# Splitting weights a chunk ahead and turning modulation rows a call later in a convolution and pooling mixer

## The chip, the cores and the metric

One core of a Trainium2 chip runs the kernel in one launch. The metric is device time in microseconds (us); a smaller one is better. Engines are named as in the profile: PE (TensorE, matmuls), PEld (its weight loads), DVE (VectorE), ACT (ScalarE), POOL (GpSimd), SP (SyncE, which here issues the loads).

## The reference

Two layers of a trunk work on 768 tokens (512 latent and 256 context) of width 1024. Layer 0's mixer is a pooling branch beside a convolution branch, layer 1's an mLSTM beside grouped-query attention, and each is followed by an expert retrieval (PEER). What matters here:

```python
z = h @ w_in                                  # mixer of layer 0: 12 chunks of 128 columns
ya = multiscale_pool(z[..., :D_POOL])         # chunks 0 to 3
a, gt = jnp.split(z[..., D_POOL:], 2, -1)     # chunks 4 to 7 and 8 to 11
u = a * jax.nn.sigmoid(gt)
y = depthwise_conv(u, conv_w)                 # 31 taps along the tokens, per column
out = concat([ya, silu(layer_norm(y))], -1) @ w_out
```

Every sub-layer has a modulation (shift, scale and gate), a linear map of the conditioning vector: for each layer 12 pieces of 512 outputs, each `silu(c) @ mod_w` plus a bias. The layer input h of a mixer is `x * (1 + scale) + shift`.

## The kernel before, in words

Matrices in float32 are split into a high and a low part (`split`: ScalarE casts the high part, L295; VectorE subtracts for the low one, L296), and a product is three matmuls: high by low, high by high, low by high.

**First mixer** (`mixer0`, L425). `zchunk(m)` loads one 128-column weight chunk of 512 KB (`load_chunk`, L311; SP), splits it into `c_hi` and `c_lo`, and runs its 48 matmuls (`mm_chunk`), 24 of 512 and 24 of 256 tokens, into the PSUM tile `zps`. A loop over g = 0 to 3 (L514) runs a value chunk (pa) and a gate chunk (pg), the sigmoid `sg` on ScalarE (L520) and their product `upad` on VectorE (L522, L523). Then the taps of that g start as a generator (`taps`, L466). For g = 1 and 2 a tap is one VectorE operation (L472); for g = 0 it is a scaled copy `ctap` on ScalarE (L476) and an add on GpSimd (L477). The fourth g's taps run on PE later (`taps_pe`, L480, matmuls with scaled identity matrices `cdh` and `cdl`). A second loop (L532) runs the four pool chunks z, copied by ScalarE into `g_acc` and `g_h`; `pooled` (L550) and `taps_pe` follow. `advance(6)` (L499) is called once per chunk, and lets each running tap generator issue up to 4 (g = 0) or 6 (g = 1, 2) taps.

**Modulation** (`mod_piece`, L180). A piece is a load of 2 MB (`modw`), 32 matmuls of two rows by 128 columns (the profile counts each as two records) into `modp`, four ScalarE copies into `mrow` (L195), a PE transpose of `mrow` into `modt` (L71), and a VectorE add of the bias into `modT` (L199), for scales also L201. `modp` and `modt` share two PSUM buffers. The first four pieces come before the first mixer, two more after each g, one after each z chunk: 16 of the 24. Weights for these are held in a ring of three `modw` buffers.

**Second mixer** (`mixer1`, L1108). The last eight pieces are placed by `mod()` (L1308) between the groups of the projection (`tps`, weights `t_hi`, `t_lo`) and the four query chunks (`qps`). Their weights come in quarters of 512 KB through `g_acc` and `g_h`. Queries are normed on DVE, POOL and ACT (`rny`, `qdup`) and transposed on PE (`qaps`).

**Order.** A scheduler places each engine's instructions within the bounds of the program; PSUM buffers, tile rings and the calls of `issue_after` set which of them can move. Each engine then runs its own list in order.

Of the kernel before, what the change touches and what calls it, by code (L numbers as in the profile page):

```python
# [9 lines left out]
F32 = mybir.dt.float32  # L10
# [5 lines left out]
OP = mybir.AluOpType  # L16
AX = mybir.AxisListType

P = 128
D = 1024  # L20
KB = D // P
NLAT, NCTX = 4, 2
NTOK = (NLAT + NCTX) * P
# [30 lines left out]
        "eq": (1.2, 0, 0), "tree": (.8, 0, 0), "gates": (1.0, 0, .6), "none": (0, 0, 0)}  # L54
NEG = -3.0e38
CONV_W = 31
ROPE_F = 16


# [15 lines left out]
def kernel(tc, a, out):  # L75
    nc = tc.nc
    V, S, G, PE, SP = nc.vector, nc.scalar, nc.gpsimd, Tracked(nc.tensor), nc.sync
# [19 lines left out]
    def kt(shape, name, dt=F32):  # L97
        return kp.tile(shape, dt, name=name)


    small = kt([P, a["smalls"].shape[1]], "small")
# [11 lines left out]
    cT, mod_bT = part(KB, 2), part(2, 48)  # L113
    pool_ls, conv_w = part(4), part(4, CONV_W)
    conv_b, conv_g, conv_lb = part(4), part(4), part(4)
    ln_gT, ln_bT = part(3, KB), part(3, KB)

    iota, row = kt([P, P], "iota"), kt([P, 1], "row")
    G.iota(iota, pattern=[[1, P]], base=0, channel_multiplier=0, allow_small_or_imprecise_dtypes=True)
    G.iota(row, pattern=[[1, 1]], base=0, channel_multiplier=1, allow_small_or_imprecise_dtypes=True)  # L120
    ident = kt([P, P], "ident")
# [46 lines left out]
    anchor, loaded, copied = [None], [None], [None]  # L168


    scT = kt([P, KB, 2], "scT")
    S.activation(scT, cT, AF.Silu)
    modT = [kt([P, 48, 2], f"modT{l}") for l in range(2)]
    mrow = [kt([P, P], f"mrow{i}") for i in range(2)]
    mcount = [0]
    for r in mrow:
        G.memset(r, 0.0)

    def mod_piece(l, j, w, pp, tag="small", bufs=2, after=None, queue=SP):

        nb = KB // len(w)
        ps = pp.tile([P, P], F32, name="modp", tag=tag, bufs=bufs)
        for k in range(KB):
            if k % nb == 0:
                with tc.issue_after(after.ins) if after is not None else nullcontext():
                    queue.dma_start(w[k // nb], a["mod_w"][l, j, :, k:k + nb])
            for g in range(4):
                PE.matmul(ps[32 * g:32 * g + 2], scT[:, k, :], w[k // nb][:, k % nb, g * P:(g + 1) * P],
                          start=k == 0, stop=k == KB - 1, tile_position=(0, 32 * g))
        mcount[0] += 1  # L190
        row = mrow[mcount[0] % 2]
        pt = pp.tile([P, P], F32, name="modt", tag=tag, bufs=bufs)
        for g in range(4):
            r = slice(32 * g, 32 * g + 2)
            S.copy(row[r], ps[r])  # L195
        PE.transpose(pt, row, ident)
        pt = pt.rearrange("p (g r) -> p g r", r=32)[:, :, :2]
        dst = modT[l][:, 4 * j:4 * j + 4, :]
        V.tensor_tensor(dst, pt, mod_bT[:, l, 4 * j:4 * j + 4].unsqueeze(2).to_broadcast([P, 4, 2]), op=OP.add)  # L199
        if j // 2 in (1, 4):  # L200
            V.tensor_scalar_add(dst, dst, 1.0)  # L201

    def gate_rows(dst, l, blk, s, wp, pp, tag="small", bufs=2):
        for h in range(2):
# [96 lines left out]
    def mm_chunk(ps, wh, wl, hh, hl, n):  # L301

        for k in range(KB):
            for w, h, first, last in ((wh, hh, k == 0, False), (wh, hl, False, False), (wl, hh, False, k == KB - 1)):
                for o, ln in spans(n):
                    PE.matmul(ps[:, o:o + ln], w[:, k], h[:, k, o:o + ln], start=first, stop=last)
# [5 lines left out]
    def load_chunk(src, wp, bufs=2, tag="c", rbufs=3, parts=()):  # L312
        raw = wp.tile([P, KB, P], F32, name="c_raw", tag=tag + "_raw", bufs=rbufs)
        loaded[0] = SP.dma_start(raw, src)
        wh, wl = parts.pop() if parts else chunk_parts(wp, bufs, tag)
        anchor[0] = split(wh, wl, raw)
        return wh, wl
# [109 lines left out]
    def mixer0(gt):  # L427
        with ExitStack() as es:
# [4 lines left out]
            ppS = pool(e3, "m0psS", 1, PSUM)  # L433
            ppB = pool(e3, "m0psB", 1, PSUM)
            e4 = ExitStack()
            wp = pool(e4, "m0w")
            ea = ExitStack()
            mw = pool(ea, "m0mod", side="right")
            cacc = xp.tile([P, 4, 783], F32, name="cacc")
            hh = wp.tile([P, KB, NTOK], F32R, name="h1h")  # L440
            hl = wp.tile([P, KB, NTOK], F32R, name="h1l")
            segs = ((0, 0, 512), (527, 512, 256))

            def mods(*js):
                for j in js:
                    mod_piece(*divmod(j, 12), [mw.tile([P, KB, 512], F32, name="modw", bufs=3)], ppS, after=loaded[0])

            mods(0, 2, 1, 3)
            for k in range(KB):
                xt = wp.tile([P, NTOK], F32, name="xt", bufs=4)  # L450
                SP.dma_start(xt, a["xT"][:, k])
# [5 lines left out]
            def big():  # L457
                return ppB.tile([P, NTOK], F32, name="zps", tag="big", bufs=3)

            def zchunk(m):  # L460
                wh, wl = load_chunk(a["ab_w_in"][m], wp, 2, "c", 2)
                ps = big()
                mm_chunk(ps, wh, wl, hh, hl, NTOK)
                return ps

            def taps(g, up):  # L466

                V.tensor_scalar(cacc[:, g], up[:, 0:783], conv_w[:, g, 0:1], conv_b[:, g:g + 1],
                                op0=OP.mult, op1=OP.add)
                for k in range(1, CONV_W):  # L470
                    if g in (1, 2):
                        V.scalar_tensor_tensor(cacc[:, g], up[:, k:k + 783], conv_w[:, g, k:k + 1], cacc[:, g],  # L472
                                               op0=OP.mult, op1=OP.add)
                    else:
                        ct = cp.tile([P, 783], F32, name="ctap", bufs=2)
                        S.activation(ct, up[:, k:k + 783], AF.Copy, scale=conv_w[:, g, k:k + 1])  # L476
                        G.tensor_tensor(cacc[:, g], cacc[:, g], ct, op=OP.add)  # L477
                    yield

            def taps_pe(g, uh, ul):  # L480

                ps = big()
                for k in range(CONV_W):
                    w = conv_w[:, g, k:k + 1]
# [12 lines left out]
            running = []  # L497
# [14 lines left out]
                for o in (0, 520, 784):  # L512
                    G.memset(zp[:, o:o + 8], 0.0)
            for g in range(4):  # L514
                pa = zchunk(4 + g)
                advance(6)
                pg = zchunk(8 + g)
                advance(6)
                sg = wp.tile([P, NTOK], F32, name="sg")
                S.activation(sg, pg, AF.Sigmoid)  # L520
                up = ups[g]
                V.tensor_tensor(up[:, 15:527], pa[:, :512], sg[:, :512], op=OP.mult)  # L522
                V.tensor_tensor(up[:, 542:798], pa[:, 512:], sg[:, 512:], op=OP.mult)  # L523
                if g < 3:
                    running.append((taps(g, up), (4, 6, 6)[g]))
                else:
                    uh = cp.tile([P, 813], F32R, name="uph", bufs=1)
                    ul = cp.tile([P, 813], F32R, name="upl", bufs=1)
                    split(uh, ul, up)
                    us.append((g, uh, ul))  # L530
                mods(2 * g + 4, 2 * g + 5)
            for g in range(4):  # L532
                ps = zchunk(g)
                zp = gs[g]
                S.copy(zp[:, 8:520], ps[:, :512])
                S.copy(zp[:, 528:784], ps[:, 512:])
                advance(6)
                mods(12 + g)
            e4.close()
            ea.close()  # L540
            op = Operand(NTOK, "opa", NL)
            e5 = ExitStack()
            wp = pool(e5, "m0p")
# [45 lines left out]
            wp = pool(e5, "m0n")  # L589
# [28 lines left out]
            wp = pool(es, "po")  # L618
            pp = pool(es, "po_ps", 1, PSUM)
# [489 lines left out]
    def mixer1(op, pre, wp, ready, gt):  # L1109
        order = ((4, 5, 0, 1, 2, 3), (5, 4, 3, 2, 1, 0))  # L1110
        with ExitStack() as es:
# [23 lines left out]
            with ExitStack() as e2:  # L1135
                pr = pool(e2, "m1p")
                pp = pool(e2, "m1_ps", 1, PSUM)
# [165 lines left out]
                        else:  # L1303
                            hold(prep_q(t, c0 // DH, ps[:, :n]))

                mods = iter([(1, j) for j in range(4, 12)])

                def mod():  # L1308
                    ws = [gt[x][:, 0].rearrange("p (k n) -> p k n", n=512) for x in ("acc", "h")] * 2
                    mod_piece(*next(mods), ws, pp, "sm", 3)  # L1310

                group("gkv", 0, *CD_FIRST[0], ready[0], (0, 4, 1, 5, 2, 3))
                if MO == 0:
                    seen_groups.add("k")
                group("qa", 0, *CD_FIRST[1], ready[1])
                seen_groups.add("k")
                mod()
                mod()
                group("qa", 256, 1792, 256)
                mod()  # L1320
                group("k", 0, 0, 256)
                mod()
                group("k", 256, 256, 256)
                mod()
                for m in range(H4):
                    wh, wl = load_chunk(a["cd_w_q"][m], wp, 2, "t", 2)
                    ps = pp.tile([P, NL], F32, name="qps", tag="tps", bufs=5)
                    mm_chunk(ps, wh, wl, op.hi, op.lo, NL)
                    S.copy(qT[:, m], ps)
                    if m % 2:  # L1330
                        mod()
                for q_ in later + gates:
                    for _ in q_:
                        pass
                later.clear()
                group("v", 0, 512, 256)
                mod()
                group("v", 256, 768, 256)
                group("o", 0, 1024, 256)
                group("o", 256, 1280, 256)  # L1340
# [3 lines left out]
            op = Operand(NL, "opc", len(DENSE[1]) * P)  # L1344
            with ExitStack() as e2:
                wp = pool(em, "m1b")
                wa = pool(e2, "m1t", side="right")
                SM = [wp.tile([P, NLAT, 2, 2, P], F32, name=f"sm{d}") for d in range(2)]
                pp = pool(e2, "m1b_ps", 1, PSUM)
# [266 lines left out]
    with ExitStack() as es:  # L1616
        gt = gather_state(0, es)
        op = mixer0(gt)
        nxt = peer(op, 0, gt, x_d[1])
    with ExitStack() as es:  # L1620
        gt = gather_state(1, es)
        op = mixer1(*nxt, gt)
# [75 lines left out]
```

## Time and profile before

| | us |
|---|---|
| median of three runs | 3821.45 (3821.12 to 3821.5) |
| the profiled execution's own time | 3821.29 |
| its span in the profile | 3819.5 |
| first mixer, second chunk's end to the start of the PE taps | 147.2 (53.0 to 200.2) |
| second mixer, the projections | 165.4 (2118.5 to 2283.9) |
| PE busy, share of the span | 96% |
| mean granted clock of PE, of full speed | 0.983 |

A time in a timeline counts from the start of the span. Busy time is work of an engine; an engine that runs its list in order waits where the next instruction's input or buffer is not there. In square brackets stands the idle time ahead of an instruction and what ended it. The two expert retrievals take most of the span and are not touched.

### The profile page before, as it was taken

What the parts mean: (1) busy time and instruction counts of PE and PEld (TensorE: products, weight loads), DVE (VectorE), ACT (ScalarE), POOL (GpSimd) and SP (SyncE); (2) the same over time, 40 slices, a digit from 0 to 9 for tenths busy, and PEclk for the clock granted to TensorE, in tenths of its full rate; (3) what the DMA queues carried; (4) which work ended last, traced back from release to release, by engine and by line L of the source; (5) the groups of instructions that cost most, each with busy time, mean ns of one, the idle gap of its engine ahead of it and who ended that gap; (6) DMA issues with size and microseconds to landing.
All of it is one profiled execution on the core that took longest, in us unless ns stands there. A gap on an engine that the chain in (4) does not pass through costs nothing. (4 is left out here: it accounts for less than half of the span.)

```text
span 3819.5 us, 57323 instructions
## 1 busy us (share of the span) xinstructions
PE 3653.0 (96%) x20375; PEld 3165.7 (83%) x20375; DVE 3101.9 (81%) x6574; ACT 1838.8 (48%) x3234; POOL 1715.0 (45%) x1213
## 2 busy tenths in 40 slices
PE   7789999999999999999998999899999999999998
PEld 5668788788888778888887889789999999888776
DVE  4977899999999778889886517588988887688778
ACT  4342322388888733323224434433358998333332
POOL 3300155444454467888860203103422223687773
PEclk9899999999999999999999999899999999999999
DMA  8323499899999989999983430157978889899885
GB/s 318 137 86 123 163 324 329 303 333 360 378 347 356 371 321 346 358 376 362 356 330 129 136 111 1 67 205 270 313 263 320 311 298 342 302 328 331 315 318 195
DMA packets 376286, 1044.01 MB, mean 273 GB/s; under 512 B 32192, under 2 KB 171840, under 8 KB 346560
## 3 DMA queue, kind: packets, MB, share of 16 engines
q1 hardware_dynamic: 263824, 632.15, 45.3%
q0 software_dynamic: 112032, 407.95, 29.8%
q8 instruction: 160, 2.62, 0.3%
q14 instruction: 126, 1.03, 0.1%
q10 hardware_dynamic: 144, 0.26, 0.0%
HBM read 915.98 MB, written 124.26 MB: 272 GB/s over the span
## 5 line engine op out<-in xcount | busy, mean ns | idle before, releaser
L662 POOL DMA_INDIRECT g_row<-in_peer_u_dram,g_idx x384 | 524.1, 1365 | 824.0 <-DVE g_row L666 324.6
L662 POOL DMA_INDIRECT g_row<-in_peer_v_dram,g_idx x384 | 580.4, 1512 | 298.8 <-DVE g_acc L670 148.7
L295 ACT CAST c_hi<-c_raw 128x1024 fp32r<-128x1024 f32 x304 | 318.5, 1048 | 595.7 <-PE ups L67 453.5
L296 DVE TENSOR_TENSOR v_lo<-v_raw,v_hi 128x1024 fp32r<-128x1024 f32 x256 | 412.3, 1610 | 209.0 <-ACT v_hi L295 208.9
L295 ACT CAST v_hi<-v_raw 128x1024 fp32r<-128x1024 f32 x256 | 269.3, 1052 | 646.6 <-DMA v_raw<-in_peer_v_dram 359.6
L1062 POOL TENSOR_TENSOR w<-ag,gg 128x512 f32<-128x512 f32 (+1 forms) x256 | 452.3, 1767 | 273.3 <-DVE w_lo L296 224.9
L67 PE MATMUL res<-v_hi,w_hi 128*128 128x512 f32 x1792 | 555.3, 390 | 10.2 <-ACT w_hi L295 10.0
L67 PE MATMUL res<-v_lo,w_hi 128*128 128x512 f32 x1792 | 555.0, 390 | 0.6
L67 PE MATMUL res<-v_hi,w_lo 128*128 128x512 f32 x1792 | 554.2, 390 | 0.0
L670 DVE SCALAR_TENSOR_TENSOR g_acc<-g_row,g_act,g_acc 128x1024 f32<-128x1024 f32 x381 | 531.3, 1395 | 2.9
L296 DVE TENSOR_TENSOR c_lo<-c_raw,c_hi 128x1024 fp32r<-128x1024 f32 x304 | 373.1, 1228 | 175.5 <-ACT c_hi L295 156.9
L666 DVE SCALAR_TENSOR_TENSOR g_row<-g_row,g_h 128x1024 f32<-128x1024 f32 x384 | 487.9, 1287 | 4.7 <-DMA g_row<-in_peer_u_dram,g_idx 4.7
L67 PE MATMUL ups<-opah,c_hi 128*128 128x512 f32 x1152 | 458.2, 398 | 3.7 <-ACT c_hi L295 3.7
L67 PE MATMUL ups<-opah,c_lo 128*128 128x512 f32 x1152 | 451.4, 393 | 5.5 <-DVE c_lo L296 5.5
L67 PE MATMUL ups<-opal,c_hi 128*128 128x512 f32 x1152 | 452.0, 392 | 0.0
L67 PEld LDWEIGHTS res<-v_hi,w_hi 128*128 128x128 f32 x1792 | 336.5, 188 | 82.5 <-ACT w_hi L295 13.0
L67 PE MATMUL ups<-opch,c_hi 128*128 128x384 f32 x1152 | 393.1, 341 | 4.8 <-ACT c_hi L295 4.8
L67 PEld LDWEIGHTS res<-v_lo,w_hi 128*128 128x128 f32 x1792 | 336.5, 188 | 73.1 <-DVE v_lo L296 3.8
L67 PEld LDWEIGHTS res<-v_hi,w_lo 128*128 128x128 f32 x1792 | 336.6, 188 | 71.0 <-DVE w_lo L296 1.2
L67 PE MATMUL ups<-opch,c_lo 128*128 128x384 f32 x1152 | 387.9, 337 | 3.7 <-DVE c_lo L296 3.7
L67 PE MATMUL ups<-opcl,c_hi 128*128 128x384 f32 x1152 | 386.6, 336 | 0.0
L811 ACT ACTIVATE o<-iota,ijT 128x128 f32<-128x128 f32 x896 | 292.0, 401 | 0.2
(483 smaller groups left out, 6641.5 us busy)
## 6 DMA issues: line engine op xcount, KB each, us to landing
c_raw<-in_uT_dram SPq DMA_DIRECT2D x256, 512.0 KB
v_raw<-in_peer_v_dram SPq DMA_DIRECT2D x128, 1024.0 KB
G_d<-stage SPq DMA_DIRECT2D x56, 1024.0 KB
modw<-in_mod_w_dram SPq DMA_DIRECT2D x16, 2048.0 KB
c_raw<-in_peer_wq_dram SPq DMA_DIRECT2D x64, 512.0 KB
gg<-G_d SPq DMA_DIRECT2D x64, 512.0 KB
A_d<-at SPq DMA_DIRECT2D x120, 256.0 KB
ag<-A_d SPq DMA_DIRECT2D x30, 1024.0 KB
```

What stands on the lines that cost most here:

```text
L67: self.last = self.engine.matmul(*args, **kw)
L295: copied[0] = S.copy(hi, src)
L296: return V.tensor_tensor(lo, src, hi.bitcast(F32), op=OP.subtract)
L662: G.indirect_dma_start(out=row, out_offset=None, in_=a[f"peer_{'uv'[tab]}{l}"], in_offset=bass.IndirectOffsetOnAxis(ap=idx[i][:, s:s + 1], ...
L666: V.scalar_tensor_tensor(row, row, 1.0, h, op0=OP.mult, op1=OP.mult, accum_out=w)
L670: V.scalar_tensor_tensor(acc, row, w, acc, op0=OP.mult, op1=OP.add)
L811: S.activation(o1[:, i], iota, AF.Abs, bias=tr[:, 0, n0 + i:n0 + i + 1])
L1062: G.tensor_tensor(w.rearrange("p (t m) -> p t m", m=TG), ag[:, i], gg[:, :, (c + i) % GG, :], op=OP.mult)
```

## The change

The weight parts `c_hi` and `c_lo` get three buffers instead of two (`CB`), and `zload` loads and splits the weight of the next chunk right after a chunk's matmuls, ahead of the taps that are issued at that place. All tap generators issue 4 taps at a call. `mod_pieces` handles one or two pieces in one PSUM tile, with a row tile `mrow` for each, and returns a function that transposes them and adds the bias; it is called at the next call of `mods`, one chunk later. Per g there are three pieces (one after the value chunk, two after the gate chunk), after each z chunk two. So all 24 are in the first mixer, and `mod()` with its quarter loads is gone from the second.

```diff
+CB = 3
...
-    def mod_piece(l, j, w, pp, tag="small", bufs=2, after=None, queue=SP):
+    def mod_pieces(js, room, pp, queue, after=None):
+        ps = pp.tile([P, 2, P], F32, name="modp", bufs=1)
+        for i, j in enumerate(js):
+            w = room()
+            with tc.issue_after(after.ins) if after is not None else nullcontext():
+                queue.dma_start(w, a["mod_w"][j // 12, j % 12])
+            for k in range(KB):
+                for g in range(4):
+                    PE.matmul(ps[32 * g:32 * g + 2, i], scT[:, k, :], w[:, k, g * P:(g + 1) * P],
+                              start=k == 0, stop=k == KB - 1, tile_position=(0, 32 * g))
+        for i, j in enumerate(js):
+            for g in range(4):
+                r = slice(32 * g, 32 * g + 2)
+                S.copy(mrow[i][r], ps[r, i])
+        def turned():
+            pt = pp.tile([P, 2, P], F32, name="modt", bufs=1)
+            for i, j in enumerate(js):
+                PE.transpose(pt[:, i], mrow[i], ident)
+            for i, j in enumerate(js):
+                l, j = divmod(j, 12)
+                src = pt[:, i].rearrange("p (g r) -> p g r", r=32)[:, :, :2]
+                dst = modT[l][:, 4 * j:4 * j + 4, :]
+                V.tensor_tensor(dst, src, mod_bT[:, l, 4 * j:4 * j + 4].unsqueeze(2).to_broadcast([P, 4, 2]), op=OP.add)
...
+        return turned
...
+            unturned = []
             def mods(*js):
-                for j in js:
-                    mod_piece(*divmod(j, 12), [mw.tile([P, KB, 512], F32, name="modw", bufs=3)], ppS, after=loaded[0])
-            mods(0, 2, 1, 3)
+                while unturned:
+                    unturned.pop(0)()
+                if js:
+                    unturned.append(mod_pieces(js, lambda: mw.tile([P, KB, 512], F32, name="modw", bufs=3), ppS, SP,
+                                               loaded[0]))
+            for j in (0, 2, 1, 3):
+                mods(j)
+            mods()
...
-            def zchunk(m):
-                wh, wl = load_chunk(a["ab_w_in"][m], wp, 2, "c", 2)
+            zorder = [4, 8, 5, 9, 6, 10, 7, 11, 0, 1, 2, 3]
+            zparts = []
+            def zload():
+                if zorder:
+                    zparts.append(load_chunk(a["ab_w_in"][zorder.pop(0)], wp, CB, "c", 2))
+            def zchunk():
                 ps = big()
-                mm_chunk(ps, wh, wl, hh, hl, NTOK)
+                mm_chunk(ps, *zparts.pop(0), hh, hl, NTOK)
+                zload()
                 return ps
+            zload()
...
             for g in range(4):
-                pa = zchunk(4 + g)
+                pa = zchunk()
                 advance(6)
-                pg = zchunk(8 + g)
+                mods(4 + 3 * g)
+                pg = zchunk()
                 advance(6)
...
-                    running.append((taps(g, up), (4, 6, 6)[g]))
+                    running.append((taps(g, up), 4))
...
-                mods(2 * g + 4, 2 * g + 5)
+                mods(3 * g + 5, 3 * g + 6)
             for g in range(4):
-                ps = zchunk(g)
+                ps = zchunk()
...
                 advance(6)
-                mods(12 + g)
+                mods(16 + 2 * g, 17 + 2 * g)
+            mods()
...
-                mods = iter([(1, j) for j in range(4, 12)])
-                def mod():
-                    ws = [gt[x][:, 0].rearrange("p (k n) -> p k n", n=512) for x in ("acc", "h")] * 2
-                    mod_piece(*next(mods), ws, pp, "sm", 3)
...
-                mod()
-                mod()
                 group("qa", 256, 1792, 256)
-                mod()
                 group("k", 0, 0, 256)
-                mod()
                 group("k", 256, 256, 256)
-                mod()
...
-                    if m % 2:
-                        mod()
...
-                mod()
```

On VectorE, from the second g's gated product on (`upad_328` before, `upad_334` after, with its taps `cacc`), the list before reads:

```order
L522 TENSOR_TENSOR upad_328<-zps,sg 128x512
L523 TENSOR_TENSOR upad_328<-zps,sg 128x256
L468 TENSOR_SCALAR cacc<-upad_328,small 128x783
L472 SCALAR_TENSOR_TENSOR cacc<-upad_328,small,cacc 128x783
L199 TENSOR_TENSOR modT_77<-modt,small 128x8
L472 SCALAR_TENSOR_TENSOR cacc<-upad_328,small,cacc 128x783 x3
L199 TENSOR_TENSOR modT_77<-modt,small 128x8
L472 SCALAR_TENSOR_TENSOR cacc<-upad_328,small,cacc 128x783 x6
L296 TENSOR_TENSOR c_lo<-c_raw,c_hi 128x1024
L472 SCALAR_TENSOR_TENSOR cacc<-upad_328,small,cacc 128x783 x7
```

and with the change:

```order
L547 TENSOR_TENSOR upad_334<-zps,sg 128x512
L548 TENSOR_TENSOR upad_334<-zps,sg 128x256
L302 TENSOR_TENSOR c_lo<-c_raw,c_hi 128x1024
L492 TENSOR_SCALAR cacc<-upad_334,small 128x783
L496 SCALAR_TENSOR_TENSOR cacc<-upad_334,small,cacc 128x783 x4
L203 TENSOR_TENSOR modT_77<-modt,small 128x8 x2
L205 TENSOR_SCALAR modT_77<-modT_77 128x8 x2
L295 TENSOR_TENSOR fold_g<-modT_77,small 128x16
L302 TENSOR_TENSOR c_lo<-c_raw,c_hi 128x1024
L496 SCALAR_TENSOR_TENSOR cacc<-upad_334,small,cacc 128x783
```

The adds into `modT` now come as a pair behind four taps, and the split of the next weight (`c_lo`) ahead of the first tap.

On PE, at the end of a pool chunk of the first mixer, the list before reads (`zps` is the chunk's output, `modp` a modulation piece, `modt` the transpose):

```order
L67 MATMUL zps<-h1h,c_lo 128x256
L67 MATMUL modp<-modw,scT 2x128 x32
L67 MATMUL zps<-h1h,c_hi 128x512
L67 MATMUL zps<-h1h,c_hi 128x256
L67 MATMUL zps<-h1l,c_hi 128x512
L67 MATMUL zps<-h1l,c_hi 128x256
L67 MATMUL zps<-h1h,c_lo 128x512
L71 MATMUL modt<-ident,mrow_79 128x128
```

and with the change:

```order
L68 MATMUL zps<-h1h,c_lo 128x256
L72 MATMUL modt<-ident,mrow_79 128x128
L72 MATMUL modt<-ident,mrow_80 128x128
L68 MATMUL modp<-modw,scT 2x128 x32
L68 MATMUL zps<-h1h,c_hi 128x512
L68 MATMUL modp<-modw,scT 2x128 x32
L68 MATMUL zps<-h1h,c_hi 128x256
L68 MATMUL zps<-h1l,c_hi 128x512
```

Before, a piece is followed, five matmuls on, by its own transpose; now the transposes of an earlier call stand ahead of two pieces.

On PE, in the projections of the second mixer (`tps`), behind the two transposes of the values (`kaps`), the list before reads:

```order
L71 MATMUL kaps<-ident,vx 128x128 x2
L67 MATMUL modp<-g_acc,scT 2x128 x8
L67 MATMUL modp<-g_h,scT 2x128 x8
L67 MATMUL tps<-t_hi,opbh_18323 128x256
L67 MATMUL tps<-t_lo,opbh_18323 128x256
L67 MATMUL tps<-t_hi,opbl_18324 128x256
```

and with the change:

```order
L72 MATMUL kaps<-ident,vx 128x128 x2
L68 MATMUL tps<-t_hi,opbh_18645 128x256
L68 MATMUL tps<-t_lo,opbh_18645 128x256
L68 MATMUL tps<-t_hi,opbl_18646 128x256
L68 MATMUL tps<-t_hi,opbh_18645 128x256
```

The quarters of the piece are gone, and the group's matmuls follow at once. Outside the first mixer's chunks and the second mixer's projections the order is the same on all five queues; the number of PE's instructions is the same.

## Rows read from the trace of the kernel before

**Rows 1.** The page, part 1: busy us (share of the span) and instructions of TensorE
```profile
PE 3653.0 (96%) x20375; PEld 3165.7 (83%) x20375; DVE 3101.9 (81%) x6574; ACT 1838.8 (48%) x3234; POOL 1715.0 (45%) x1213
```

**Rows 2.** Windows, first mixer: from:to us, length; busy (count) by engine; clock; DMA share; GB/s
```profile
33.70:53.00 19.30, 18.95 (x97) 15.98 (x98) 9.94 (x16) 6.33 (x7) 0.00 (x0) 0.89 1.02 418
53.00:82.00 29.00, 25.50 (x300) 21.07 (x299) 7.16 (x10) 19.24 (x27) 23.74 (x12) 1.00 0.58 227
82.00:126.00 44.00, 28.06 (x302) 22.59 (x303) 43.32 (x31) 17.25 (x31) 30.51 (x13) 0.81 0.39 139
126.00:160.00 34.00, 26.33 (x230) 21.62 (x229) 34.00 (x32) 10.99 (x18) 17.00 (x6) 0.85 0.65 254
160.00:200.20 40.20, 39.79 (x433) 32.98 (x431) 24.24 (x31) 8.62 (x22) 0.00 (x0) 0.99 0.20 70
```

**Rows 3.** Timeline, PE, first mixer: start, us, line, operation, count [idle before <-releaser]
```profile
91.99 0.52 PE L67 MATMUL zps<-h1h,c_lo 128*128 128x512 f32 x2
...
124.71 0.45 PE L71 MATMUL modt<-ident,mrow 128*128 128x128 f32 x1 [10.99 <-DVE modT L199]
125.17 0.84 PE L67 MATMUL zps<-h1h,c_lo 128*128 128x512 f32 x2
...
168.52 0.33 PE L71 MATMUL modt<-ident,mrow 128*128 128x128 f32 x1
...
198.32 1.93 PE L67 MATMUL modp<-modw,scT 128*2 128x128 f32 x64
...
200.18 0.61 PE L67 MATMUL zps<-uph,cdh 128*128 128x512 f32 x2
```

**Rows 4.** Waits, PE, 53 to 200.2 us: waiting <- waited for: us, times, longest
```profile
PE modt L71 <- ACT mrow L195: 16.1, 6, 5.7
PE modt L71 <- DVE modT L199: 11.0, 1, 11.0
```

**Rows 5.** Groups, VectorE, 82.4 to 184.3 us: busy us, mean ns, idle before
```profile
L472 DVE SCALAR_TENSOR_TENSOR cacc<-upad,small,cacc 128x783 f32<-128x783 f32 x60 | 86.5, 1466 | 0.9
```

**Rows 6.** Timeline, VectorE, first mixer
```profile
81.83 0.68 DVE L522 TENSOR_TENSOR upad<-zps,sg 128x512 f32<-128x512 f32 x1
...
124.41 0.16 DVE L199 TENSOR_TENSOR modT<-modt,small 128x8 f32<-128x8 f32 x1
...
129.08 7.65 DVE L472 SCALAR_TENSOR_TENSOR cacc<-upad,small,cacc 128x783 f32<-128x783 f32 x8
...
136.64 1.22 DVE L296 TENSOR_TENSOR c_lo<-c_raw,c_hi 128x1024 fp32r<-128x1024 f32 x1
...
137.78 16.33 DVE L472 SCALAR_TENSOR_TENSOR cacc<-upad,small,cacc 128x783 f32<-128x783 f32 x7
...
179.97 4.25 DVE L472 SCALAR_TENSOR_TENSOR cacc<-upad,small,cacc 128x783 f32<-128x783 f32 x4
...
203.16 0.97 DVE L561 TENSOR_TENSOR psum<-psum,pinv 128x776 f32<-128x776 f32 x1 [0.24 <-DMA pinv<-in_pinv_dram]
```

**Rows 7.** Windows, second mixer: all work, then the modulation pieces (tile modp) alone
```profile
2118.50:2283.90 165.40, 156.83 (x1550) 138.75 (x1550) 56.25 (x157) 52.07 (x120) 21.43 (x44) 1.00 0.40 134
2118.50:2283.90 165.40, 18.52 (x512) 10.87 (x512) 8.19 (x32) 1.00 0.40 134
```

**Rows 8.** Waits, PE, second mixer, 2118.5 to 2283.9 us
```profile
PE modp L67 <- DMA g_acc<-in_mod_w_dram: 4.9, 9, 1.1
PE modt L71 <- ACT mrow L195: 1.5, 6, 0.6
```

**Rows 9.** The chain of waits, second mixer, 2083 to 2290 us: start, us, group, count
```profile
2197.08 5.92 PE qps L67 x26
...
2248.87 34.99 PE tps L67 x296
```

**Rows 10.** Timeline, VectorE, second mixer
```profile
2125.30 0.42 DVE L296 TENSOR_TENSOR qdup<-rny,qdup 128x256 fp32r<-128x256 f32 x1
```

**Rows 11.** Timeline, GpSimd, first mixer
```profile
57.40 36.02 POOL L477 TENSOR_TENSOR cacc<-cacc,ctap 128x783 f32<-128x783 f32 x16 [54.96 <-DVE cacc L468]
```

More of the change, by code (lines that the diff above doesn't have):

```diff
@@ L174 @@
     mrow = [kt([P, P], f"mrow{i}") for i in range(2)]
-    mcount = [0]
     for r in mrow:
         G.memset(r, 0.0)
-    def mod_piece(l, j, w, pp, tag="small", bufs=2, after=None, queue=SP):
[L181 to L186, printed above, removed]
-            for g in range(4):
[L188 to L201, printed above, removed]
@@ new lines, in mod_pieces @@
+    def mod_pieces(js, room, pp, queue, after=None):
[9 more added lines that the diff above has]
+        for i, j in enumerate(js):
+            for g in range(4):
+                r = slice(32 * g, 32 * g + 2)
[9 more added lines that the diff above has]
+                V.tensor_tensor(dst, src, mod_bT[:, l, 4 * j:4 * j + 4].unsqueeze(2).to_broadcast([P, 4, 2]), op=OP.add)
+                if j // 2 in (1, 4):
+                    V.tensor_scalar_add(dst, dst, 1.0)
+        return turned
```

## The prediction

> **What bounds the kernel now.** I read the page's busy shares, then the two stretches that the change touches, first by windows, then by waits, timelines and chain. TensorE (PE below) is busy for 96% of the span [rows 1], so an edit pays only where it takes work or waits from PE, or where the end of a stretch hangs on another engine.
>
> First mixer, 53.0 to 200.2 us [rows 2]. Each projection chunk is 48 matmuls, 24 pairs of 512 and 256 columns. Pairs start every .353 us, so a chunk is 24 x .353 = 8.5 us, and the chunk that ends at 53.0 leaves ten to go. In two rows the granted clock is 0.81 and 0.85, which is a mix of 2.4 and 1.2 GHz: after the wait that ended at 124.71 a pair shows .84 us, in an unbroken stretch .52 [rows 3]. The waits say what breaks the stretch: seven transposes of modulation rows stand for 16.1 + 11.0 = 27.1 us, for ScalarE's copies into mrow and, once, for VectorE's modT add [rows 4]. PE runs in order, so the chunk behind each of them stands too. VectorE is busy through 82 to 160 (43.32 of 44.0, 34.00 of 34.0) with sixty taps, 86.5 us [rows 2, 5]. The 11.0 us wait is one of its small adds that ran only at 124.41, behind taps [rows 6]. The balance of PE from 53.0: 10 chunks 85.0, 12 modulation pieces of 1.93 [rows 3] 23.2, eleven transposes at about .25 in the queue 3, waits 27.1, which makes 191.3; the 8.9 left to 200.2 is the price of the low clock, with small gaps. VectorE's taps end at 184.2 [rows 6], 16 us before the PE taps begin at 200.18 [rows 3]. So PE is the later of the two here.
>
> Second mixer, 2118.5 to 2283.9: clock 1.00, PE busy 156.83 of 165.40 us, 18.52 of it in the modulation pieces [rows 7], and it waits 4.9 us for their quarter loads and 1.5 for their copies [rows 8]. Its chain is PE's own [rows 9].
>
> **Second mixer, part by part.** Removed from PE: eight pieces, 18.52 us, eight transposes at .33 [rows 3], 2.6, and 6.4 us of waits: 27.5 at least. From the other side: the matmuls that stay go at their own pace, 864 x 34.99/296 = 102.1, 96 x 5.92/26 = 21.9 [rows 9], and I put some 7 us on the small transposes of the attention and gate work. That is 131 of the 165.4, so the pieces with all that they disturb are worth up to 34 us. ScalarE's copies and the 32 quarter loads go too, at no price: neither ends the chain. What is late next: the query transposes, which need qdup. Today qdup is ready at 2125.7 [rows 10], behind 48 matmuls of the next group and two pieces; without the pieces PE is there about 2124.2, so it waits 1.5 us. The same may come four more times; I take 6 us in all, between 0 and 10. So 34 − 6 = **28 us** gained; the ends are 27.5 − 10 = 17.5 and 34.
>
> **First mixer.** Added to PE: eight pieces, some 1.93 + .25 us each, 17.4 us (one of them falls behind the start of PE's taps, 15.3 on the path to it). Removed: the 27.1 us of waits and the 8.9 of low clock, as far as nothing new stands there. A transpose is now asked for a whole chunk after its copies, so ScalarE has over 8 us for copies of 1 us; that wait I put at zero. What can remain is VectorE, whose add for the last call must be done before the tile modt (one buffer) is written again. I walk both engines from call to call. PE: second chunk ends 54.9 (a single piece ahead of it), then 8.5 + 2.2 us after a single piece, 8.5 + 4.1 after a pair: 78.5 for the second g's gate chunk, 102.1 for the third's, 125.7 for the fourth's.
>
> VectorE starts the second g's gated product at about 80.4 (81.83 now, [rows 6]). From there: sixty taps at .956 (7.65/8, alone) 57.3, seven splits of 1.14 (from 136.64 to 137.78, [rows 6]) 8.0, products, first taps, adds and the split of the fourth g 6.8: 72.1 us. Beside a GpSimd tap one of its taps takes about 2.55 instead (16.33 for seven, [rows 6]), 1.6 more; today's 86.5 us for sixty [rows 5] are 57.3 and eighteen such tolls. GpSimd makes 1.98 us of a tap alone (23.74/12, [rows 2]); its first comes some 6 us later than now [rows 11], since two pieces' copies stand ahead of it on ScalarE. So 22 of its 30 are left at 80.4, three of which fall in VectorE's idle time: 19 x 1.6 = 30.4. The idle: taps in fours end the third g's first list at 86.1, and VectorE waits for the transposes at 91.5, 5.4 us. Sum: 80.4 + 72.1 + 30.4 + 5.4 = 188.3 for the end of its taps. The same sum for the kernel before gives 82.4 + 71 + 29 = 182.4, against 184.2 seen.
>
> Where the two meet, PE waits for modT adds behind taps twice, about 2.7 us after the fourth gate chunk and 3.1 after the second pool chunk. So PE: 54.9 + 85.0 + 18 pieces 34.7 + transposes 4 + 5.8 = 184.4; the walk with its rounding gives **185.3** for the start of its taps, 14.9 earlier. The pool stage needs VectorE too, free at 188.3; the multiplication that stands at 203.16 [rows 6] then comes at about 189.9. So the tail is **13.3 us** earlier; the ends are 6, by the dearer price of a tap pair below, and 14.9 plus the 2 us by which the check was low, 17.
>
> VectorE and GpSimd side by side are the dear item. The rows show 2.55 us for a pair of taps that take .956 and 1.98 alone, so they overlap in part. The Trainium skill ("SBUF — State Buffer", section "SBUF: two separate sides") says that the two engines' shared port pair is an exclusive lock, held for a whole instruction, and that the loser blocks fully, also a VectorE operation with two SBUF inputs against a GpSimd one that reads SBUF. By that rule a pair would cost .956 + 1.98 = 2.94, and the nineteen would add 19 x .39 = 7.4 us to VectorE's path; the trace disagrees with its 2.55, so the sum keeps the rows.
>
> Loads: the added 2 MB loads lie beside chunks. A pool chunk with its pair needs .52 + 4.2 = 4.72 MB in 12.6 us, 375 GB/s; the stretch 33.7 to 53.0 moved 418 GB/s [rows 2]. Covered, with little to spare; three buffers and a chunk of lead take up the rest. On SP the eight whole loads are issued among the chunk loads, in program order; one that waits for its buffer would hold the next chunk's load behind it, and the buffer is free once the piece three before is done. The profiled execution took 3821.29 us, 0.16 below the median of the three runs; I subtract from it.
>
> **Sum.** 3821.3 − 28 − 13.3 = **3780.0 us**. By the two pairs of ends this forecast's own range is 3821.3 − 34 − 17 = 3770 to 3821.3 − 17.5 − 6 = 3798.
>
> **The rivals.** What a measurement of this kernel can tell from no change is about 0.2%, 7.6 us; a chance stands behind each.
> - Full blocking of VectorE by GpSimd taps, as a mechanism of its own: 2.94 us a pair, the first mixer gains 5.9, **3787**. Against it the 16.33 us for seven. 0.08.
> - VectorE becomes the bound of the first mixer, because its adds are behind taps at more calls than two, and PE gains only what it loses in added pieces. Then the second mixer alone counts, **3793**. For it: two rows in which VectorE has no idle time. Against it: in 160 to 200.2 it works 24.24 of 40.2 us. 0.13.
> - The norm chain of the queries takes ten us of PE's time, and what it removes is worth its low end: −13.3 − 17.5, **3790**. 0.07.
> - The split does not run ahead, since ScalarE's c_hi stands behind four ctap copies that go at GpSimd's pace, 4 x 2.55 = 10.2 us. If that exposes half of it at eight calls, it costs 41 us and the change gives nothing: **3821**. Against it: 10.2 is less than a chunk with its call, 12.6. 0.06.
> - Slower: the loads bound the first mixer. At the mean rate of 53 to 82, 227 GB/s [rows 2], a pool chunk's 4.72 MB take 20.8 us, 8.2 more than its work, four times; a g's 7.34 MB take 32.3 against 23.3, 9 more, three times. Together 60: 3821.3 − 28 − 13.3 + 60 = **3840**. It turns slower at a rate of about 250. Against it: in that row the queues were busy for 0.58 of the time only, so the rate was what was asked for. 0.06.
>
> **How the numbers follow.** The forecast has 0.60. Faster by over 0.2%: forecast and the first three rivals, 0.88. Within 0.2%: 0.06. Slower: 0.06. The range is the forecast's own and the rivals at 3787, 3790 and 3793, with some us for those on either side: 3765 to 3802. It leaves out the last two rivals and the tails.
>
> **What would show it.** Right: PE's taps of the first mixer begin near 185, with a granted clock of 0.95 or more from 82 to 160, no wait of modt on mrow over 1 us, and VectorE's taps end near 188. In the second mixer the stretch shrinks to about 137 us, and qaps waits for qdup for some 6. Wrong: waits of modp on modw or of zps on c_hi (loads, late split), waits of modt on modT over 5 us at several calls, a second mixer over 148 us.

## The result, and the profile after

The changed kernel takes 3778.84 us (median of four runs, 3776.67 to 3781.63), the kernel before 3821.47: a ratio of 0.9884 (95% interval 0.9872 to 0.9896), 43 us less. Forecast were 3780.0 us, 3765 to 3802. The profiled execution took 3781.63 us, the slowest of its four; its terms are compared with the sum below.

The windows of the first mixer in the changed kernel (stretch and length in us; busy us and count of PE, PEld, DVE, ACT, POOL; granted clock; DMA share; GB/s), against [rows 2]:

```profile
53.00:82.00 29.00, 29.00 (x415) 24.48 (x416) 7.74 (x13) 15.12 (x25) 16.06 (x8) 1.00 0.92 375
82.00:126.00 44.00, 42.08 (x475) 35.88 (x463) 40.14 (x29) 26.54 (x46) 38.51 (x16) 1.00 0.80 316
126.00:160.00 34.00, 29.60 (x417) 24.27 (x421) 34.00 (x33) 13.76 (x29) 14.37 (x6) 0.90 0.69 277
160.00:200.20 40.20, 39.75 (x503) 33.19 (x492) 39.87 (x58) 15.14 (x44) 0.00 (x0) 1.00 0.66 234
```

PE has 28.06 busy us of 44 before and 42.08 now, and the clock there is 1.00 instead of 0.81. In 160 to 200.2 it is VectorE that has no room left, 39.87 us of 40.2 against 24.24 (its taps fill this stretch up to 188 us, the pool stage the rest). The loads move at 375 GB/s in the first row, and no wait of PE for one is seen. The waits of PE from 53 to 186 us (waiting <- waited for: us in total, times, longest), against [rows 4]:

```profile
PE modt L72 <- DVE modT L203: 5.9, 1, 5.9
PE modt L72 <- DVE modT L205: 0.4, 1, 0.4
```

27.1 us have become 6.3, and none is for ScalarE's copies. On PE's timeline, the place of the wait and the start of the PE taps (200.18 in [rows 3]):

```profile
130.01 0.44 PE L72 MATMUL modt<-ident,mrow 128*128 128x128 f32 x1 [5.92 <-DVE modT L203]
130.38 6.46 PE L68 MATMUL modp<-modw,scT 128*2 128x128 f32 x128
...
183.79 1.93 PE L68 MATMUL modp<-modw,scT 128*2 128x128 f32 x64
185.65 0.61 PE L68 MATMUL zps<-uph,cdh 128*128 128x512 f32 x2
```

The two pieces behind the wait take 6.46 us; elsewhere one takes 1.93. That is the low clock again, once, after PE stood idle for 5.92 us. VectorE's timeline, against [rows 6]:

```profile
98.22 1.85 DVE L296 TENSOR_TENSOR fold_b<-modT,small 128x16 f32<-128x16 f32 x1
...
140.39 17.42 DVE L496 SCALAR_TENSOR_TENSOR cacc<-upad,small,cacc 128x783 f32<-128x783 f32 x8
...
175.76 12.43 DVE L496 SCALAR_TENSOR_TENSOR cacc<-upad,small,cacc 128x783 f32<-128x783 f32 x12
...
189.96 0.96 DVE L587 TENSOR_TENSOR psum<-psum,pinv 128x776 f32<-128x776 f32 x1
```

Its taps end at 188.2, the multiplication that stood at 203.16 is at 189.96, 13.2 us earlier.

The projections of the second mixer ended at 2283.9 and end at 2238.6. They are counted from the end of the same two transposes, behind which the first piece stood (in the kernel before, then in the changed one):

```profile
2118.15 0.44 PE L71 MATMUL kaps<-ident,vx 128*128 128x128 f32 x2
```
```profile
2101.36 0.44 PE L72 MATMUL kaps<-ident,vx 128*128 128x128 f32 x2
```

From there on the projections took 165.4 us [rows 7] and take 136.9, which is 28.5 us less. Their window, and PE's waits in it, against [rows 8]:

```profile
2101.70:2238.60 136.90, 132.18 (x1030) 126.52 (x1030) 52.37 (x144) 43.54 (x88) 17.38 (x43) 1.00 0.15 47
```
```profile
PE qaps L72 <- DVE qdup L302: 2.9, 2, 1.5
PE qaps L72 <- DVE rr L224: 1.7, 1, 1.7
```

The waits for quarter loads and copies are gone, and 4.6 us of waits for the query norms have come (0.9 before).

13.2 + 28.5 = 41.7 us, against 39.7 in the two profiled executions. What lies between is seen when the starts of the same matmul are compared in both traces. The first output matmul of the first mixer is 14.5 us earlier:

```profile
257.77 0.81 PE L67 MATMUL wops<-woh,opah 128*128 128x512 f32 x2
```
```profile
243.26 0.81 PE L68 MATMUL wops<-woh,opah 128*128 128x512 f32 x2
```

At the start of the second mixer's projections it is 16.8 us (the transposes above), after them 45.3, after the attention 41.1, at the end 39.7. The 2.3 us more between the first mixer's output and the second mixer lie in what stands between the two, the first expert retrieval above all, which the change doesn't touch. The 4 us given back in the attention lie in these windows, first the kernel before, then the changed one at the same work, and third the changed kernel in another execution (its second run, on another chip, below):

```profile
2420.00:2430.00 10.00, 6.89 (x36) 5.71 (x35) 6.12 (x11) 5.56 (x9) 0.00 (x0) 0.66 0.64 216
2430.00:2444.00 14.00, 11.71 (x77) 9.90 (x78) 10.42 (x19) 8.12 (x13) 0.00 (x0) 1.00 0.24 76
```
```profile
2375.00:2385.00 10.00, 7.11 (x30) 6.30 (x31) 5.37 (x7) 5.47 (x8) 0.00 (x0) 0.51 0.63 217
2385.00:2399.00 14.00, 12.56 (x65) 11.22 (x64) 8.72 (x15) 7.13 (x11) 0.00 (x0) 0.62 0.23 76
```
```profile
2375.00:2385.00 10.00, 7.44 (x40) 6.28 (x39) 7.23 (x14) 5.66 (x9) 0.00 (x0) 0.72 0.49 181
2385.00:2399.00 14.00, 13.01 (x87) 11.16 (x87) 8.96 (x15) 8.08 (x14) 0.00 (x0) 1.00 0.24 76
```

The clock stayed at its low level longer in the first execution of the changed kernel, and not in the other, where the end is 47.6 us earlier than in the kernel before's profile: so it is not the change in itself that gives these 4 us back.

### The profile page after: what moved, and what is told of

The parts are those of the page before. It is cut to its first block, busy times and chain, and to the rows that moved or that the text cites. A ratio compares the mean times of both kernels' runs of the same rounds, so it can differ in the third digit from the quotient of the medians.

```text
span 3779.9 us, 57257 instructions
## 1 busy us (share of the span) xinstructions
PE 3640.1 (96%) x20375; PEld 3165.4 (84%) x20375; DVE 3108.3 (82%) x6574; ACT 1837.1 (49%) x3234; POOL 1707.5 (45%) x1213
## 4 chain that ended last, share of the span: by engine, by line
PE 67%; DVE 10%; ACT 6%; issue 5%; DMA 5%; POOL 4%; SPq 1%; DVEq 0%; POOLq 0%; ACTq 0%
PE ups L68 32%; PE res L68 18%; PE gps L68 4%; PE tps L68 3%; PE zps L68 2%; POOL w L1088 2%; DMA v_raw<-in_peer_v_dram 2%; PE wops L68 2%; POOL g_row L688 2%; SPq L883 1%; ACT o L837 1%; DMA ag<-A_d 1%; ACT stage L846 1%; DVE cacc L496 1%; PE mlps L68 1%
## 5 line engine op out<-in xcount | busy, mean ns | idle before, releaser
L302 DVE TENSOR_TENSOR v_lo<-v_raw,v_hi 128x1024 fp32r<-128x1024 f32 x256 | 419.9, 1640 | 206.9 <-ACT v_hi L301 206.9
```

The source lines that it names most:

```text
L302: return V.tensor_tensor(lo, src, hi.bitcast(F32), op=OP.subtract)
```

## The experiments

Each ratio is to the kernel before on the same chip, whose medians there were 3824.92, 3825.14 and 3822.38 us. Two theories stand against each other in the first mixer: that VectorE's taps set its end (the walk's result), or that PE sets it.

**Eight pieces left in the second mixer.**

```diff
-                mods(16 + 2 * g, 17 + 2 * g)
+                mods()
...
                 group("qa", 0, *CD_FIRST[1], ready[1])
+                mod()
+                mod()
```
(and the other six calls of `mod()` as before)

> The changed kernel with its eight last modulation pieces back between the second mixer's projections (quarter loads, as before), the first mixer otherwise as changed. If VectorE's taps set the end of the first mixer, taking eight pieces off PE there brings the tail at most 2 us earlier, and the second mixer gets back the 165 us of before: about 3805 us. If PE sets the end of the first mixer, the missing eight pieces bring it some 13 us earlier, and the whole is about 3792 us.

Measured: 3810.82 us, 0.9965 (0.9951 to 0.9979). VectorE's timeline has the pool multiplication where the changed kernel has it:

```profile
190.08 0.96 DVE L613 TENSOR_TENSOR psum<-psum,pinv 128x776 f32<-128x776 f32 x1
```

So with eight pieces less, 15 us of PE's work, PE's taps begin earlier (178.18 against 185.65), but the pool stage comes no earlier: the eight pieces ride there free, and VectorE sets that end. The price of these pieces in the second mixer is 0.9965 − 0.9884 of 3821.5, 31 us (28.5 by the windows above).

**Pieces moved, nothing else.**

```diff
                 pa = zchunk(4 + g)
                 advance(6)
+                mods(4 + 3 * g)
...
-                mods(2 * g + 4, 2 * g + 5)
+                mods(3 * g + 5, 3 * g + 6)
...
-                mods(12 + g)
+                mods(16 + 2 * g, 17 + 2 * g)
...
-                mod()
```
(of the kernel before; all calls of `mod()` go)

> The kernel before with all 24 pieces in the first mixer at the places of the change, and nothing else of it: each piece is turned at once, weights are split behind the taps, taps go in 4, 6 and 6. The second mixer gains 28 us by either theory. If eight more pieces cost PE only their own work, 17 us, the whole is about 3811 us; if each also brings a wait of some 3 us as the pieces of before do (27.1 us over 12), the first mixer loses about 40 us, and the whole is 3825 to 3835 us.

Measured: 3811.29 us, 0.9968 (0.9957 to 0.998). PE's taps begin at 219.85 instead of 200.18. Its waits from 53 to 205 us:

```profile
PE zps L67 <- DVE c_lo L296: 16.6, 5, 9.8
PE modt L71 <- ACT mrow L195: 8.5, 5, 3.7
PE zps L67 <- ACT c_hi L295: 1.7, 1, 1.7
```

26.8 us of waits, as many as the kernel before, but of another kind: the weight split is now late. The first mixer's output matmuls come 18.7 us later than in the kernel before, which is the eight pieces' own work (17 us expected) and little more; the second mixer gains 28.5. By the ratios a move alone gets 12 of the 44 us; the rest comes from what was done around the pieces.

**Turned at once.**

```diff
-                    unturned.append(mod_pieces(js, lambda: mw.tile([P, KB, 512], F32, name="modw", bufs=3), ppS, SP,
-                                               loaded[0]))
+                    mod_pieces(js, lambda: mw.tile([P, KB, 512], F32, name="modw", bufs=3), ppS, SP,
+                               loaded[0])()
```

> The changed kernel, but each call's transposes and adds follow its own pieces at once. If the waits of the transposes for ScalarE's copies are what the later call removes, PE waits again in each of the 11 calls behind copies and taps, 20 us or more in all on modt from 53 us on, the granted clock falls to 0.9 or below between 82 and 160 us, the PE taps begin near 200 us, and the time is 3790 to 3800 us. If VectorE's taps set the end anyway and hide these waits, it stays within 4 us of 3779.

Measured: 3787.46 us, 0.9909 (0.989 to 0.9927). PE's taps begin at 200.43, the granted clock is 0.88 and 0.90 in the two stretches, and its waits are:

```profile
PE modt L72 <- ACT mrow L193: 15.5, 8, 6.8
```

Less than the 20 us and the 3790 us or more that were expected, but of the kind named: without the later call the change loses about 9 us.

**Taps in fours or not.**

```diff
-                    running.append((taps(g, up), 4))
+                    running.append((taps(g, up), (4, 6, 6)[g]))
```

> The changed kernel with the taps of g = 1 and 2 in sixes, as before. The waits on modT, 6.3 us in the changed kernel, grow to 15 us or more, since up to twelve VectorE taps stand ahead of an add. If VectorE sets the end of the first mixer, its idle time from 86.9 to 90.6 us is filled, and the stretch ends 0 to 4 us earlier. If PE sets the end, the waits cost 8 us or more.

Measured: 3793.58 us, 0.9917 (0.9901 to 0.9934). Waits of PE, and the start of its taps:

```profile
PE modt L72 <- DVE modT L203: 15.4, 1, 15.4
PE modt L72 <- DVE modT L205: 4.4, 1, 4.4
```
```profile
202.74 0.61 PE L68 MATMUL zps<-uph,cdh 128*128 128x512 f32 x2
```

The waits came as said, and the stretch ended later, not 0 to 4 us earlier: the theory that VectorE alone sets the end fell here. Its taps still end at 188.7, but PE, which stood 15.4 us behind taps (the clock from 126 to 160 is 0.80), is now the later one. The two are close: whichever the edit delays sets the end. Taken out of the change, the fours cost about 13 us, the most of the parts.

**Split late.**

```diff
-CB = 3
+CB = 2
...
             def zchunk():
+                zload()
                 ps = big()
                 mm_chunk(ps, *zparts.pop(0), hh, hl, NTOK)
-                zload()
                 return ps
-            zload()
```

> The changed kernel with two buffers for the weight parts and the split issued where a chunk's matmuls are, behind the taps, as before. The prediction gave the split ahead no price, since PE of the kernel before never waits for c_hi or c_lo: by that it stays within 3 us of 3779. If the split ahead is needed now, since copies for the GpSimd taps stand before c_hi on ScalarE, PE waits 2 to 5 us at several of the eight chunks behind them, and the time is 3789 us or more.

Measured: 3783.21 us, 0.9892 (0.9875 to 0.9908). One row of PE's waits and one of its timeline:

```profile
PE zps L68 <- DVE c_lo L302: 13.1, 3, 9.6
```
```profile
132.71 1.01 PE L68 MATMUL zps<-h1h,c_lo 128*128 128x512 f32 x2 [9.57 <-DVE c_lo L302]
```

The split is late behind VectorE's taps, not ScalarE's copies; the pool multiplication is at 197.62, 7.7 us later. (The third buffer goes together with the early split; the two were not tried apart.) The whole showed only part of it, so this one and two others were run again on one chip.

> The changed kernel again, beside the next two on one chip. About 0.988 of the kernel before; the first mixer 17 to 18 us earlier at its end than the kernel before, the second 27 to 28 us more.

> The kernel of the late split again. In its first profile the first mixer ended 8 us later than the changed kernel's, in the times of the whole only 3 us showed. If the split ahead is worth what the profile showed, the median is 6 to 9 us above the changed kernel's on the same chip; if the 8 us are given back later, within 3 us.

Measured: the changed kernel 3777.76 us, 0.9884 (0.9863 to 0.9905), the late split 3782.45 us, 0.9896 (0.9878 to 0.9914), so 4.7 us apart in the medians, while the intervals overlap. PE's waits for c_lo are 12.6 us again, and the multiplication stands at 191.71 and 198.09, 6.4 us apart. Against the kernel before, the changed kernel's output matmuls are here 11.6 us earlier, its second mixer begins 16.0 earlier (17 to 18 were expected), and its projections gain 28.5 again. The late split lies between its two expectations: the loss in the first mixer is shown, its size in the whole is not settled closer than 3 to 7 us.

**A second half for modt.**

```diff
-            pt = pp.tile([P, 2, P], F32, name="modt", bufs=1)
+            if turns[0] is None:
+                turns[0] = pp.tile([P, 2, 2, P], F32, name="modt", bufs=1)
+            pt = turns[0][:, turns[1] % 2]
+            turns[1] += 1
```

> The changed kernel with two halves for modt, so that a transpose may be written while VectorE has not yet read the one of the call before. PE's waits on modT, 6.3 us, and the low clock behind the first of them go, some 9 us of PE. If VectorE's taps set the end of the first mixer, they still end near 188 us and the time is within 2 us of the changed kernel's. If PE sets it, the time falls by 6 to 9 us.

Measured: 3778.92 us, 0.9878 (0.9862 to 0.9895). It tells nothing on the question: PE still waits 5.8 and 1.4 us on modT, so the edit didn't take the wait away. Perhaps that is because both halves belong to one tile, whose readers the wait still covers; no run here shows it.

**The first g's later taps on VectorE.**

```diff
-                    if g in (1, 2):
+                    if g in (1, 2) or k > 8:
```

> The changed kernel with the first g's taps from the ninth on as VectorE operations, so that GpSimd has 8 instead of 30 and is idle from about 81 us on. If a GpSimd tap costs VectorE 1.6 us beside it, VectorE loses 19 tolls, 30 us, and gains 22 taps of .956, 21 us: its taps end about 9 us earlier, near 179 us, PE's wait on modT shrinks, and the time is about 3770 us. If the tolls don't lie on the path that sets the end (PE sets it), the 21 us of added taps change nothing or come out as a longer wait: 3779 to 3790 us.

Measured: 3766.1 us, 0.9848 (0.9831 to 0.9864), below both kernels. The windows, VectorE's tap group from 79 to 178 us and two places of its timeline:

```profile
82.00:126.00 44.00, 44.00 (x544) 37.82 (x540) 40.52 (x53) 10.86 (x30) 0.00 (x0) 1.00 0.82 320
126.00:160.00 34.00, 34.00 (x494) 29.28 (x487) 34.00 (x44) 11.54 (x32) 0.00 (x0) 1.00 0.91 355
```
```profile
L496 DVE SCALAR_TENSOR_TENSOR cacc<-upad,small,cacc 128x783 f32<-128x783 f32 x82 | 79.7, 1030 | 0.3
```
```profile
92.66 0.16 DVE L205 TENSOR_SCALAR modT<-modT 128x8 f32<-128x8 f32 x1
...
165.49 12.44 DVE L496 SCALAR_TENSOR_TENSOR cacc<-upad,small,cacc 128x783 f32<-128x783 f32 x12
...
179.91 0.96 DVE L587 TENSOR_TENSOR psum<-psum,pinv 128x776 f32<-128x776 f32 x1
```

82 taps take 79.7 us; in the changed kernel sixty take 81.3 beside GpSimd's. VectorE's taps end at 177.9, 10.3 us earlier, with 22 more of them on it. PE has no idle time in the two stretches, its clock is 1.00, and its taps begin at 177.36. The run on the same chip as the two above:

> The kernel with the first g's later taps on VectorE again: 10 to 15 us below the changed kernel on the same chip, of which 10 in the first mixer, where PE has no wait over 1 us.

Measured: 3763.88 us, 0.9848 (0.9829 to 0.9868), 13.9 us below the changed kernel's median there.

**The same in the kernel before.**

```diff
-                    if g in (1, 2):
+                    if g in (1, 2) or k > 8:
```

> The kernel before with the first g's taps from the ninth on as VectorE operations. VectorE's taps end some 9 us earlier than 184 us, but PE begins its taps 16 us after that already, so by the theory that PE's waits set this kernel's first mixer the gain comes only through these waits: those for ScalarE's copies (16.1 us), which stand behind copies for GpSimd taps, should fall to 5 us or less, and the time to 3805 to 3815 us. If VectorE's adds behind up to sixteen taps at a call hold PE instead, waits on modT grow and the time is 3821 us or more.

Measured: 3800.07 us, 0.9939 (0.9919 to 0.9959), 23 us less, more than expected. PE's two largest waits from 53 to 205 us:

```profile
PE modp L67 <- DVE modT L199: 4.4, 1, 4.4
PE modt L71 <- ACT mrow L195: 3.6, 4, 1.3
```

The 16.1 us for ScalarE's copies [rows 4] have become 3.6, and the clock from 82 to 126 is 1.00. So most of the waits that the change goes around came with GpSimd's taps (through ScalarE's copies for them or VectorE's toll beside them, which go together here). On ScalarE of the kernel before, the copies of the rows stand behind a copy for a GpSimd tap, which waits for GpSimd:

```profile
83.64 0.95 ACT L476 ACTIVATE ctap<-upad,small 128x783 f32<-128x783 f32 x1 [1.32 <-POOL cacc L477]
84.50 1.04 ACT L195 COPY mrow<-modp 2x128 f32<-2x128 f32 x4
```

Behind these copies ended PE's longest wait for ScalarE, 5.7 us. Not all of them came this way: one of 3.8 us ended behind a cast for which ScalarE had itself waited for VectorE. This one edit brings the first mixer's output matmuls 16.4 us earlier than in the kernel before, more than the whole change does there (14.5 and 11.6 in its two profiles, with eight pieces more in the stretch).

## Why the prediction was right, point by point

- *Second mixer, 34 − 6 = 28.* 28.5 us by the windows, and 28.4 to 28.7 in every other profile of a kernel without the eight pieces there. The new waits of qaps were 4.6 us, against 6. One of the two kinds was not named: for rr, a step earlier in the same norm chain.
- *First mixer, 13.3 at the pool multiplication.* 13.2. The walk gave 185.3 for the PE taps (185.65 seen), 188.3 for the end of VectorE's (188.2), 189.9 for the multiplication (189.96). That it agrees so closely is luck in part. In the second profile of the same kernel these places are 187.4, 189.9 and 191.7, so the tail's term is there 11.5. And in the first, errors cancelled: VectorE began the second g's product at 78.91 instead of 80.4 and waited 3.65 us instead of 5.4, so that with the 72.1 us of work some 33.5 us are left for the tolls, not 30.4 (about 21 of them, not nineteen).
- *Waits on modT, 2.7 and 3.1.* 5.9 and 0.4: the sum held (6.3 against 5.8; 7.4 in the second profile), not the places. VectorE stood further behind at the fourth gate chunk; what PE lost there it did not lose again at the second pool chunk.
- *8.9 us of low clock go.* Not all: behind the 5.92 us wait two pieces took 6.46 us instead of 2 x 1.93 = 3.9, and the clock from 126 to 160 was 0.90 (with 1.00 before it, the 0.95 that was asked for from 82 to 160 is just met). The step that credited the whole is off by some 3 us, and VectorE's later end covered it.
- *VectorE beside GpSimd, 1.6 a tap.* In the eight taps of 17.42 us (17.34 up to the start of the next instruction) six GpSimd taps lie: (17.34 − 8 x .956)/6 = 1.6, the same price. With GpSimd idle, VectorE's taps end 10.3 us earlier, against 9. But "they overlap in part" is too mild: fold_b, 0.17 us alone, took 1.85 beside a GpSimd tap, 1.7 more. A short operation pays what a long one pays. The price is 1.6 to 1.7 us, not the 1.98 us between GpSimd's taps. The Trainium skill ("SBUF — State Buffer", section "SBUF: two separate sides") calls the port pair that the two engines share an exclusive lock, and not a bandwidth split. The trace agrees in kind, since the toll doesn't grow with VectorE's operation; but the prediction's sum by the rule, 7.4 us more on VectorE, was too high here.
- *The rivals.* Loads: 375 GB/s moved and no wait. The late split was put on ScalarE's copies, for which PE waited once, 1.7 us, and only where the pieces were moved and nothing else; without the split ahead it comes from VectorE's taps, 12.6 to 13.1 us of waits in two profiles. The prediction gave the split ahead no term of its own, and it has one, of 6 to 8 us in the first mixer.
- *VectorE as the bound.* At the end it is (eight pieces less changed nothing), but by a little: PE's taps began 2.5 us before VectorE's ended. Taps in sixes turned it round.
- *The sum.* 41.3 us were forecast. The two parts measured 14.5 + 28.5 = 43.0 in the first profile, up to the first mixer's output, and 11.6 + 28.5 = 40.1 in the second, and the median fell by 43. So the account holds to some 2 us. That the median lies 1.2 us from the forecast is luck: the untouched retrievals and the attention move by several us from one execution to the next.

What stays open: where the gain between the first mixer's output matmuls and the second mixer comes from, 2.3 us in the first profile and 4.4 in the second. The code there is the same. All twelve other profiles are 2.3 to 6.6 us shorter in this stretch than the one profile of the kernel before, also that of the kernel before with nothing but its taps moved (4.5); so that one execution may have been slow there. A second profile of the kernel before was not taken.

## What to carry to other kernels

Where two engines are nearly level, work for the earlier one can be taken in for nothing only if no instruction of it stands behind another engine's queue: turn a result one call later, split the next operand ahead of the long operations, and cut these into shorter runs. By the ratios, moving pieces alone got 12 of 44 us here, and the change loses 9 and 13 us without two of the other parts, and some 5, whose size is not settled, without the third. And before work is spread to GpSimd, price what it takes from VectorE: here the GpSimd adds that ran beside VectorE's taps cost it some 31 us, since without them its taps end 10.3 us earlier with twenty-two more of them on it (at .956 us, 21).

## What the runs showed of the hardware

- A VectorE operation of 0.17 us took 1.85 beside a GpSimd add of 128 x 783 in float32, and a tap of 0.96 took about 2.55: a fixed toll of 1.6 to 1.7 us for each GpSimd operation, not a share of the time. GpSimd pays less: nine of its adds beside VectorE's work took 22.00 us, 2.44 each, and eight almost alone 16.61, 2.08 each.
- In the attention, the mean granted clock was 0.62 in one execution and 1.00 in another at the same work; some 4 us hung on it. The same kernel ran between 3773.69 and 3781.63 us, on two chips.
